# A two-layer hybrid decoder trunk in float32 on one core: the elementwise work leaves GpSimd, norm sums and gate results are placed between weight splits, and two raw weight buffers are added

## The chip, the core and the metric

The kernel runs on one core of a Trainium2 chip. A core has a matrix engine (TensorE, PE; its weight loads are listed apart as PEld), a vector engine (VectorE, DVE), an engine for activations, casts and copies (ScalarE, ACT) and a general engine (GpSimd, POOL). SyncE (SP) here only issues DMA transfers. Each engine works through its own list of instructions in a fixed order and waits, by semaphores, for results of others. The metric is device time in microseconds for one launch.

## The reference

The input is `x` of 256 positions by 2048 channels, float32. Two layers follow one another; layer 0 mixes tokens with a state-space scan (SSD), layer 1 with forgetting attention (FoX). In both, the rest is the same:

```python
h = h + rmsnorm(mix, norm_mix_post[i])
ff = swiglu(rmsnorm(h, norm_ffn_pre[i]), ffn_w_gate[i], ffn_w_up[i], ffn_w_down[i])
h = h + rmsnorm(ff, norm_ffn_post[i])
pe = rmsnorm(p[i] @ ple_w_proj[i], ple_norm[i])
h = h + jax.nn.sigmoid(h @ ple_w_gate[i]) * pe
```

`swiglu` is `(silu(h @ w_gate) * (h @ w_up)) @ w_down` with 5632 hidden channels; `rmsnorm` divides by the root of the mean square over the channels and multiplies by a gain. The per-layer embedding (PLE) has 256 channels. Every weight is read once.

## The kernel before

**Layout.** Channels lie on the 128 partitions, positions along the free axis: `h` is 16 tiles (chunks) of 128 x 256. A float32 product is made of three passes. A weight `raw` is split into a high part `wh` (a cast on ACT, L174) and a low part `wl = raw - wh` (DVE, L176); an activation `x` likewise into two halves that lie beside each other (`split`: the high half on ACT, L261 or L264, the low half on DVE, L262 or L265). For each weight tile PE then does one pass of `wh` over both halves (512 columns, L233) and one of `wl` over the high half (256 columns, L235). `gather` (L256 on ACT, L257 on DVE) adds the two halves of an accumulator.

**Stages and units.** All weights are cut, ahead of time, into a list of stages of 128 x 640 to 128 x 1024. `emit_stage` makes a stage's DMA, cast and low part. `wh` and `wl` have four buffers each (`WB`), so stage i+4 can be cast only when PE has left stage i; `raw` has four (`RAWB`). `unit` runs one group of output tiles over all chunks of the contraction, looks `LOOK` = 2 stages ahead, and after each stage takes one entry (`pops`) from the queue `bg` of deferred work. At a unit's end it calls `evac` for each accumulator. The scheduler then fixes the order on each engine; `issue_after` pins an instruction behind another on that order. An accumulator has one of six buffers, so a unit of six tiles takes all of them.

**FFN.** `tail` runs per layer. Behind the mixer, `post_norm` makes the norm's scale. The first gate unit (stages 242 to 257 in layer 0, six tiles, 768 wide, one chunk a stage) is run while `mk_update` makes its inputs: per chunk c a scaled product `sg` or `pn` (L414), `h[c] += ` that (L422 on DVE, L424 on POOL for even c from 4), the split into `x` (L264, L265), and the square of `h` (ACT, L273) added to `ssb` on POOL (L274). At its end `mk_r` makes the norm scale of `ssb`: a matmul with ones (L280), `pow` on POOL (L287), a diagonal (`dg`, L293), a matmul (L296) that spreads it to `rwide` and `rwide2`. Each gate tile is then gathered into `sg`, multiplied by `rwide2` (L487), passed through tanh (L489), multiplied (L490) and scaled by `rwide` (L491). The up unit follows (stages 258 to 273), whose tiles are gathered into `g`, multiplied by `sg` (L506) and split into `a`, the input of the down product. Sums `ssp` of the squares of `pp`, the embedding's projection, run between stages by `bg`.

**PLE.** After the down products a second update without gain makes the gate product's input in its first unit. The four units have 6, 4, 4 and 2 tiles (`OUT0`). `e3` closes a tile as soon as its unit ends: gather, tanh (L553), `pp` times `rpe` on POOL (L537), `(1+th)*pp` (L555), residual into `h` (L556); then in layer 0 the split `xb` for the next layer and the square's sum on POOL, in layer 1 the output's DMA on SP.

**After layer 0** come five units for the values of FoX with tokens on the output partitions (`tok`); the first ends with `mk_r` on `ssb`.

Of the kernel before, what the change touches and what calls it, by code (L numbers as in the profile page):

```python
# [56 lines left out]
def tile_trunk(ctx, tc, a, out):  # L57
# [99 lines left out]
    def emit_stage(a_ins=None, v_ins=None):  # L157
# [15 lines left out]
        with after(a_ins):  # L173
            A.copy(out=wh[:, :kc * n], in_=raw[:, :kc * n])  # L174
        with after(v_ins):
            V.tensor_tensor(out=wl[:, :kc * n], in0=raw[:, :kc * n],  # L176
                            in1=wh.bitcast(F32)[:, :kc * n], op=sub)
# [90 lines left out]
    def sumsq(acc, src, first, eng=None):  # L268
        if first:
            return A.activation(acc, src, AF.Square)  # L270
        else:
# [1 line left out]
            mark[0] = r = A.activation(sq, src, AF.Square)  # L273
            (eng or V).tensor_tensor(out=acc, in0=acc, in1=sq, op=add)  # L274
            return r

# [124 lines left out]
    def mk_update(new, m, wpost, wpre, xs):
# [15 lines left out]
        def up(c):  # L417
            if c == 0:
                chain(lambda: scaled(0))
            e = G if H_POOL_EVERY and c >= 3 and c % H_POOL_EVERY == 0 else V  # L420
            if e is V:
                chain(lambda: V.tensor_tensor(out=h[c], in0=h[c], in1=ts[c], op=add))  # L422
            else:
                G.tensor_tensor(out=h[c], in0=h[c], in1=ts[c], op=add)  # L424
# [42 lines left out]
    def tail(i, mpx, m, pp, mk_next):  # L467
# [3 lines left out]
        with ExitStack() as st:  # L471
# [7 lines left out]
            def ev_g(t, acc):  # L479
                if first[0]:  # L480
                    bg.append(noop)
                    for c in range(8):
                        bg.append(lambda c=c: late_ssp(pp, c))
                    first[0] = False
                sg = new_sg()
                gather(acc, sg)
# [44 lines left out]
        def mkpe():  # L531
            rs = rstd_small(ssp, D)
            rstd_wide(rs, rpe)
            V.tensor_scalar(out=rpe, in0=rpe, scalar1=0.5, scalar2=None, op0=mult)

        def mkpp(c):
            G.tensor_tensor(out=pp[c], in0=pp[c], in1=rpe, op=mult)  # L537

        def ssq2():
            for c in range(8, NCH):  # L540
                late_ssp(pp, c, G)

        c_sep = NCH - OUT0[-1]

        def e3(t, acc, c0):
            c = c0 + t
# [9 lines left out]
            V.scalar_tensor_tensor(out=h[c], in0=pe, scalar=col(f"ple{i}", c), in1=h[c], op0=mult,  # L556
                                   op1=add)
# [538 lines left out]
```

## Time and profile before

| | us |
|---|---|
| median of 3 runs | 2797.61 (2797.36 to 2799.33) |
| profiled execution | 2800.33 |
| its span | 2798.5 |
| PE busy | 2768.2 (99%) |
| DVE busy | 1926.0 (69%) |
| ACT busy | 1484.8 (53%) |
| POOL busy | 183.5 (7%), 236 instructions |

A profile is of one execution; its span begins at the first instruction on the core, its time is that of the whole launch. In a group's row stand line, engine, operation, output and inputs, shape and count, then busy time, mean of one in ns, and the idle time just ahead with what ended it. In a timeline's row stand start, duration and instruction, with the idle time ahead in brackets and its releaser where there was one. A window's row gives busy time (and the number of instructions) of PE, PEld, DVE, ACT and POOL, the share of full clock that PE was granted, the DMA engines' share and GB/s. Ends of matmuls are modelled, so times of PE are best read from start to start.

### The profile page before, as it was taken

How to read it: one execution, taken by the hardware profiler on the slowest of the kernel's cores; microseconds unless marked ns; L12 is line 12 of the kernel's file. 1: busy time of each engine (PE TensorE's matmuls, PEld its weight loads, DVE VectorE, ACT ScalarE, POOL GpSimd, SP SyncE). 2: the span in 40 equal slices, each digit the busy share in tenths (PEclk: the TensorE clock that was granted, in tenths of full speed). 3: DMA queues.
4: the chain of work that ended last, by engine and by line, in shares of the span. 5: the costliest groups of instructions: out<-in, count | busy, mean ns of one | idle time of the engine just before them, and what ended most of it. 6: DMA issues, size and time to landing. Idle time of an engine off the chain costs nothing.

```text
span 2798.5 us, 43191 instructions
## 1 busy us (share of the span) xinstructions
PE 2768.2 (99%) x16306; PEld 2447.5 (87%) x16306; DVE 1926.0 (69%) x3033; ACT 1484.8 (53%) x2455; POOL 183.5 (7%) x236
## 2 busy tenths in 40 slices
PE   9999999999999999999999999999999999999999
PEld 8888888889788888888897998888888888888888
DVE  8888888855966645666669656766866545666577
ACT  6587676644654444444446544555654444445454
POOL 2000000000300000000005000000200000000022
PEclk9999999999999999999999999999999999999999
DMA  7666665565566656666555676655666556656545
GB/s 235 189 197 183 194 191 177 158 202 180 161 201 189 192 191 188 188 180 194 194 168 167 189 207 191 178 161 166 181 189 192 192 190 187 195 172 204 192 153 176
DMA packets 262512, 520.09 MB, mean 186 GB/s; under 512 B 17392, under 2 KB 42128, under 8 KB 262304
## 3 DMA queue, kind: packets, MB, share of 16 engines
q1 hardware_dynamic: 258640, 504.96, 58.8%
q0 software_dynamic: 3520, 12.15, 1.5%
q8 instruction: 127, 2.08, 0.3%
q14 instruction: 81, 0.66, 0.1%
q10 hardware_dynamic: 144, 0.24, 0.0%
HBM read 515.10 MB, written 2.18 MB: 185 GB/s over the span
## 4 chain that ended last, share of the span: by engine, by line
PE 91%; DVE 4%; issue 4%; ACT 1%; POOL 0%; DMA 0%; DVEq 0%; ACTq 0%; POOLq 0%
PE acc L233 53%; PE acc L235 28%; PE acc L230 1%; PE acc L229 1%; PE acc L228 1%; PE acc L223 1%; PE acc L222 1%; PE acc L224 1%; PE mi L751 1%; DVE x L265 1%; DVE wl L176 1%; DVE sg L414 1%; DVE x L262 0%; DVE h L422 0%; PE mi L753 0%
## 5 line engine op out<-in xcount | busy, mean ns | idle before, releaser
L233 PE MATMUL acc<-x,wh 128*128 128x512 f32 x5008 | 1718.9, 394 | 13.7 <-DVE x L265 6.6
L176 DVE TENSOR_TENSOR wl<-raw,wh 128x1024 fp32r<-128x1024 f32 (+4 forms) x1020 | 1183.2, 1166 | 782.4 <-ACT wh L174 778.8
L174 ACT CAST wh<-raw 128x1024 fp32r<-128x1024 f32 (+4 forms) x1020 | 1006.6, 993 | 989.0 <-PE acc L233 809.9
L235 PE MATMUL acc<-x,wl 128*128 128x256 f32 x5008 | 1340.0, 283 | 7.5 <-DVE wl L176 7.5
L233 PEld LDWEIGHTS acc<-x,wh 128*128 128x128 f32 x5008 | 928.2, 188 | 209.5 <-DVE x L265 14.7
L235 PEld LDWEIGHTS acc<-x,wl 128*128 128x128 f32 x5008 | 932.5, 189 | 33.1 <-DVE wl L176 10.9
L233 PE MATMUL acc<-a,wh 128*128 128x512 f32 x1232 | 425.5, 391 | 0.0
L235 PE MATMUL acc<-a,wl 128*128 128x256 f32 x1232 | 341.9, 282 | 0.0
L233 PEld LDWEIGHTS acc<-a,wh 128*128 128x128 f32 x1232 | 229.9, 188 | 47.1
L235 PEld LDWEIGHTS acc<-a,wl 128*128 128x128 f32 x1232 | 232.6, 189 | 2.2
L233 PE MATMUL acc<-xb,wh 128*128 128x512 f32 x512 | 181.9, 396 | 0.0
L256 ACT COPY tb<-acc 128x256 f32<-128x256 f32 (+1 forms) x401 | 139.6, 369 | 38.6 <-PE acc L235 19.0
L235 PE MATMUL acc<-xb,wl 128*128 128x256 f32 x512 | 145.8, 285 | 0.0
L287 POOL TENSOR_TENSOR rs<-ms,mhalf 128x2 f32<-128x2 f32 x18 | 21.2, 1177 | 1752.8 <-DVE ms L284 1752.8
L233 PEld LDWEIGHTS acc<-xb,wh 128*128 128x128 f32 x512 | 95.9, 188 | 19.3
L235 PEld LDWEIGHTS acc<-xb,wl 128*128 128x128 f32 x512 | 96.7, 189 | 0.7 <-issue 0.2
L257 DVE TENSOR_TENSOR g<-acc,tb 128x256 f32<-128x256 f32 x204 | 78.7, 415 | 2.1 <-ACT tb L256 1.6
L233 PE MATMUL acc<-xq,wh 128*128 128x512 f32 x224 | 77.6, 390 | 0.0
L733 ACT ACTIVATE E<-ab,bias 128x128 f32<-128x128 f32 x192 | 59.8, 390 | 15.3 <-PE mi L753 14.7
L661 DVE SCALAR_TENSOR_TENSOR g<-xr,vec,g 128x256 f32<-128x256 f32 x144 | 62.4, 476 | 4.0 <-ACT g L658 3.5
L235 PE MATMUL acc<-xq,wl 128*128 128x256 f32 x224 | 62.8, 282 | 0.0
L274 POOL TENSOR_TENSOR ssb<-ssb,sqp 128x256 f32<-128x256 f32 x60 | 55.5, 925 | 61.2 <-ACT sqp L273 56.7
...
## 6 DMA issues: line engine op xcount, KB each, us to landing
raw<-down SPq DMA_DIRECT2D x176, 512.0 KB, 4.1
...
raw<-gate SPq DMA_DIRECT2D x128, 512.0 KB, 3.9
raw<-up SPq DMA_DIRECT2D x128, 512.0 KB, 4.5
...
```

The lines of the kernel that those rows point to most:

```text
L174: A.copy(out=wh[:, :kc * n], in_=raw[:, :kc * n])
L176: V.tensor_tensor(out=wl[:, :kc * n], in0=raw[:, :kc * n], in1=wh.bitcast(F32)[:, :kc * n], op=sub)
L222: PE.matmul(o, lhsT=xh, rhs=wh[:, c, :], start=st, stop=False)
L223: PE.matmul(o, lhsT=xh, rhs=wl[:, c, :], start=False, stop=False)
L224: PE.matmul(o, lhsT=x[:, 1, t * P:(t + 1) * P], rhs=wh[:, c, :], start=False, stop=sp)
L233: PE.matmul(accs[t], lhsT=wh[:, c, t * P:(t + 1) * P], rhs=x.rearrange("p a n -> p (a n)"), start=st, stop=False)
L235: PE.matmul(accs[t][:, :T], lhsT=wl[:, c, t * P:(t + 1) * P], rhs=x[:, 0, :], start=False, stop=sp)
L256: A.copy(out=tb[:np_], in_=acc[:np_, T:2 * T])
L257: V.tensor_tensor(out=o, in0=acc[:np_, :T], in1=tb[:np_], op=add)
L274: (eng or V).tensor_tensor(out=acc, in0=acc, in1=sq, op=add)
L661: V.scalar_tensor_tensor(out=c, in0=xr[:, k:k + T], scalar=col(f"conv_w{k}", cc), in1=c, op0=mult, op1=add)
L733: A.activation(E[:, i, b * P:(b + 1) * P], ab[:, i, lo:lo + P], AF.Relu, scale=-1.0, bias=bias3[:, b, h0 + i:h0 + i + 1])
```

## The change

POOL keeps `pow`, memsets and DMA issues. Its sums (`ssb`, `ssp`), its adds to `h` and its products `pp * rpe` go to DVE. The sums of the first FFN norm no longer run with the update: `late_norm` puts them in `bg` in groups of 3, 3, 3, 4 and 3, then the two steps of the scale, then the gate's tanh and products in three pairs, all into the up unit that follows the first gate unit. `paced` pins such a group behind the latest `wl`, and `turn` pins the next `wl` behind the group. The `ssp` sums of the first eight tiles move behind that unit. In PLE, `e3` only gathers into `gz` (ten buffers), and `close` is taken from `bg` in later units, one per `wl`; the last unit closes its tiles at once. The `ssb` sums for FoX run within its first value unit, two per stage. `RAWB` goes from 4 to 6; a smaller scratch for descriptors makes room.

```diff
-RAWB = 4
+RAWB = 6
+SCRATCH = 8192
...
-H_POOL_EVERY = 2
...
+    low, turn = [None], [None]
...
+        if v_ins is None:
+            v_ins, turn[0] = turn[0], None
         with after(v_ins):
-            V.tensor_tensor(out=wl[:, :kc * n], in0=raw[:, :kc * n],
-                            in1=wh.bitcast(F32)[:, :kc * n], op=sub)
+            low[0] = V.tensor_tensor(out=wl[:, :kc * n], in0=raw[:, :kc * n],
+                                     in1=wh.bitcast(F32)[:, :kc * n], op=sub)
...
-    def sumsq(acc, src, first, eng=None):
+    def sumsq(acc, src, first):
...
+            sq = tmp("sq", bufs=4)
             mark[0] = r = A.activation(sq, src, AF.Square)
-            (eng or V).tensor_tensor(out=acc, in0=acc, in1=sq, op=add)
+            last_v[0] = V.tensor_tensor(out=acc, in0=acc, in1=sq, op=add)
...
+    def sums_of(acc, src, cs, by=(2,) * 8):
+        cs = list(cs)
+        return [lambda cc=[cs.pop(0) for _ in range(n)]: [paced(sumsq, acc, src[i], i == 0)
+                                                          for i in cc] for n in by]
+
+    def paced(f, *args):
+        with tc.issue_after(low[0].ins):
+            f(*args)
+        turn[0] = last_v[0]
...
-            e = G if H_POOL_EVERY and c >= 3 and c % H_POOL_EVERY == 0 else V
-            if e is V:
-                chain(lambda: V.tensor_tensor(out=h[c], in0=h[c], in1=ts[c], op=add))
-            else:
-                G.tensor_tensor(out=h[c], in0=h[c], in1=ts[c], op=add)
+            chain(lambda: V.tensor_tensor(out=h[c], in0=h[c], in1=ts[c], op=add))
...
-            am = mark[0]
-            if wpre is not None:
-                sumsq(ssb, h[c], c == 0, G)
...
+            def late_norm():
+                f1, f2 = mk_r()
+                bg.extend(sums_of(ssb, h, range(NCH), (3, 3, 3, 4, 3)))
+                bg.extend((noop, f1, noop, noop, f2, noop))
+                for j in range(0, len(sgs), 2):
+                    bg.append(lambda ss=sgs[j:j + 2]: paced(lambda: [silu(x) for x in ss]))
...
-        def mkpp(c):
-            G.tensor_tensor(out=pp[c], in0=pp[c], in1=rpe, op=mult)
...
+        def close(c, src):
             th = tmp("th")
-            if c >= c_sep:
-                A.activation(th, acc[:, :T], AF.Tanh, scale=0.5)
-            else:
-                g0 = tmp("g0")
-                gather(acc, g0)
-                A.activation(th, g0, AF.Tanh, scale=0.5)
+            A.activation(th, src, AF.Tanh, scale=0.5)
             pe = pp[c]
+            V.tensor_tensor(out=pe, in0=pe, in1=rpe, op=mult)
             V.scalar_tensor_tensor(out=pe, in0=th, scalar=1.0, in1=pe, op0=add, op1=mult)
...
+        def e3(t, acc, c0):
+            c = c0 + t
+            gz[c] = pn.tile([P, T], F32, tag="gz", name=nm("gz"), bufs=10)
+            gather(acc, gz[c])
...
+            if u == 0:
+                bg.extend(sums_of(ssp, pp, range(8, NCH), (1, 1, 2, 1, 2, 1)))
+                bg.extend((noop, pe_small, noop, noop, pe_wide))
+            if not last:
+                for c in range(c0, c0 + n):
+                    bg.append(lambda c=c: paced(close, c, gz[c]))
+                    if c < 2:
+                        bg.append(noop)
...
+    v1, v2 = mk_r(False, rsm)
+    bg.extend(sums_of(ssb, h, range(NCH)))
     for u in range(5):
-        unit(lambda k: nxt[k], ev_v(u), tok=True, late=mk_r(False, rsm) if u == 0 else ())
+        unit(lambda k: nxt[k], ev_v(u), tok=True, pops=2 if u == 0 else 1,
+             late=(lambda: (drain(), v1()), v2) if u == 0 else ())
```

Three places show how instructions stand. The rows give line, operation, output and inputs, and shape; a number behind `wl`, `wh` and `raw` is the stage. Lines of the changed kernel differ a little: L178 is `wl`, L267 the low half of `x`, L432 the add to `h`, L426 the scaled product.

First, DVE in the FFN update of layer 0. Before (`x_715` belongs to chunk 6, `x_717` to chunk 8, whose stages are 248 and 250):

```order
L176 TENSOR_TENSOR wl249_7954<-raw249_7951,wh249_7953 128x768
L265 SCALAR_TENSOR_TENSOR x_715_7674<-h6_89,vec_79,x_715_7674 128x256
L422 TENSOR_TENSOR h7_90<-h7_90,sg_778_7932 128x256
L414 SCALAR_TENSOR_TENSOR sg_780_7958<-m0_8_6591,vec_79,rwide_138 128x256
L176 TENSOR_TENSOR wl250_7980<-raw250_7977,wh250_7979 128x768
L265 SCALAR_TENSOR_TENSOR x_716_7675<-h7_90,vec_79,x_716_7675 128x256
L414 SCALAR_TENSOR_TENSOR sg_782_7984<-m0_9_6592,vec_79,rwide_138 128x256
L265 SCALAR_TENSOR_TENSOR x_717_7676<-h8_91,vec_79,x_717_7676 128x256
```

and in the changed kernel:

```order
L178 TENSOR_TENSOR wl249_7935<-raw249_7932,wh249_7934 128x768
L267 SCALAR_TENSOR_TENSOR x_714_7673<-h5_88,vec_79,x_714_7673 128x256
L432 TENSOR_TENSOR h6_89<-h6_89,sg_772_7893 128x256
L426 SCALAR_TENSOR_TENSOR sg_773_7916<-m0_7_6590,vec_79,rwide_138 128x256
L178 TENSOR_TENSOR wl250_7958<-raw250_7955,wh250_7957 128x768
L267 SCALAR_TENSOR_TENSOR x_715_7674<-h6_89,vec_79,x_715_7674 128x256
L432 TENSOR_TENSOR h7_90<-h7_90,sg_773_7916 128x256
L426 SCALAR_TENSOR_TENSOR sg_774_7939<-m0_8_6591,vec_79,rwide_138 128x256
```

The add to `h` stands in every chunk, and the `wl` ahead of a chunk's `x` is that of two stages later (250 ahead of `x_715`, stage 248), where it was one later.

Second, the end of the first up unit of layer 0, whose last stage is 273; stage 274 is the next gate unit's first. DVE before:

```order
L176 TENSOR_TENSOR wl271_8517<-raw271_8514,wh271_8516 128x768
L176 TENSOR_TENSOR wl272_8535<-raw272_8532,wh272_8534 128x768
L176 TENSOR_TENSOR wl273_8553<-raw273_8550,wh273_8552 128x768
L176 TENSOR_TENSOR wl274_8571<-raw274_8568,wh274_8570 128x1024
L176 TENSOR_TENSOR wl275_8577<-raw275_8574,wh275_8576 128x1024
L257 TENSOR_TENSOR g0_833_8604<-acc_820_8288,tb_834_8605 128x256
L257 TENSOR_TENSOR g0_835_8611<-acc_821_8289,tb_836_8612 128x256
L506 TENSOR_TENSOR g0_833_8604<-g0_833_8604,sg_802_8234 128x256
```

DVE in the changed kernel (`sg_790` and `sg_792` are the last two of the six gate tiles, `acc_794` and `acc_795` the first two of the up unit):

```order
L178 TENSOR_TENSOR wl273_8521<-raw273_8518,wh273_8520 128x768
L485 TENSOR_TENSOR sg_790_8189<-sg_790_8189,rwide2_139 128x256
L485 TENSOR_TENSOR sg_792_8193<-sg_792_8193,rwide2_139 128x256
L488 SCALAR_TENSOR_TENSOR sg_790_8189<-th_824_8537,sg_790_8189 128x256
L259 TENSOR_TENSOR g0_826_8582<-acc_794_8197,tb_827_8583 128x256
L489 TENSOR_TENSOR sg_790_8189<-sg_790_8189,rwide_138 128x256
L259 TENSOR_TENSOR g0_828_8589<-acc_795_8198,tb_829_8590 128x256
L525 TENSOR_TENSOR g0_826_8582<-g0_826_8582,sg_782_8173 128x256
L488 SCALAR_TENSOR_TENSOR sg_792_8193<-th_825_8542,sg_792_8193 128x256
L525 TENSOR_TENSOR g0_828_8589<-g0_828_8589,sg_784_8177 128x256
L489 TENSOR_TENSOR sg_792_8193<-sg_792_8193,rwide_138 128x256
L178 TENSOR_TENSOR wl274_8549<-raw274_8546,wh274_8548 128x1024
```

and ACT in the changed kernel:

```order
L174 CAST wh276_8630<-raw276_8628 128x1024
L174 CAST wh277_8652<-raw277_8650 128x1024
L487 ACTIVATE th_824_8537<-sg_790_8189 128x256
L258 COPY tb_827_8583<-acc_794_8197 128x256
L258 COPY tb_829_8590<-acc_795_8198 128x256
L487 ACTIVATE th_825_8542<-sg_792_8193 128x256
```

The gate products of the last pair and two gathers stand ahead of `wl274`, and the tanh of that pair stands on ACT behind the casts of stages 276 and 277.

Third, DVE in layer 0's third PLE unit, in the changed kernel (before, the closes of a unit's tiles stood together at its end, with two or three of their instructions between two `wl`):

```order
L259 TENSOR_TENSOR gz_1323_15733<-acc_1301_15487,tb_1324_15734 128x256
L259 TENSOR_TENSOR gz_1325_15737<-acc_1302_15488,tb_1326_15738 128x256
L267 SCALAR_TENSOR_TENSOR xb_1236_14978<-h0_83,vec_79,xb_1236_14978 128x256
L178 TENSOR_TENSOR wl548_15670<-raw548_15667,wh548_15669 128x1024
L564 TENSOR_TENSOR pp0_1_6600<-pp0_1_6600,rpe_142 128x256
L565 SCALAR_TENSOR_TENSOR pp0_1_6600<-th_1317_15689,pp0_1_6600 128x256
L566 SCALAR_TENSOR_TENSOR h1_84<-pp0_1_6600,vec_79,h1_84 128x256
L267 SCALAR_TENSOR_TENSOR xb_1237_14979<-h1_84,vec_79,xb_1237_14979 128x256
L178 TENSOR_TENSOR wl549_15699<-raw549_15696,wh549_15698 128x1024
```

A whole close, with the split `xb` for the next layer, stands between two `wl`, and the last gathers of the unit before stand ahead of `wl548`.

More of the change, by code (lines that the diff above doesn't have):

```diff
@@ L244, in unit @@
             evac(t, accs[t])
-    mark, dmark = [None], [None]
+    mark, dmark, last_v = [None], [None], [None]
     def tmp(tag, shape=(P, T), dt=F32, bufs=2):
@@ L477, in tail, with silu @@
             first = [True]
[L479 to L486, printed above, removed]
+            def silu(sg):
                 V.tensor_tensor(out=sg, in0=sg, in1=rwide2, op=mult)
@@ L490, in ev_g @@
                 V.scalar_tensor_tensor(out=sg, in0=th, scalar=1.0, in1=sg, op0=add, op1=mult)
-                V.tensor_tensor(out=sg, in0=sg, in1=rwide, op=mult)
+                last_v[0] = V.tensor_tensor(out=sg, in0=sg, in1=rwide, op=mult)
+            def ev_g(t, acc):
+                sg = new_sg()
+                gather(acc, sg)
                 sgs.append(sg)
+                if not first[0]:
+                    silu(sg)
+            def late_norm():
[4 more added lines that the diff above has]
+                    bg.append(lambda ss=sgs[j:j + 2]: paced(lambda: [silu(x) for x in ss]))
             for half in range(2):
@@ L499, in tail, with ev_u @@
                     up = mk_update(new_sg, m, f"mix_post{i}", f"ffn_pre{i}", xs) if first[0] else None
-                    unit(lambda k: xs[k], ev_g, pre=up, late=mk_r() if first[0] else (),
-                         look=0 if first[0] else LOOK)
-                    def ev_u(t, acc, c0=c0, acts=acts):
+                    unit(lambda k: xs[k], ev_g, pre=up, look=0 if first[0] else LOOK)
+                    begun = first[0]
+                    first[0] = False
+                    if begun:
+                        late_norm()
+                    def ev_u(t, acc, c0=c0, acts=acts, begun=begun):
+                        if begun and t == 0:
+                            drain()
+                            bg.append(noop)
+                            for c in range(8):
+                                bg.append(lambda c=c: late_ssp(pp, c))
                         up = tmp("g0")
@@ L529, in tail, with pe_small, pe_wide @@
         post_norm(filler(pp, (2, 3)))
[L531 to L533 removed]
+        def pe_small():
+            r_pe.append(rstd_small(ssp, D))
+        def pe_wide():
+            rstd_wide(r_pe[0], rpe)
             V.tensor_scalar(out=rpe, in0=rpe, scalar1=0.5, scalar2=None, op0=mult)
[L536 to L553 removed]
+        r_pe = []
+        gz = {}
+        def close(c, src):
+            th = tmp("th")
+            A.activation(th, src, AF.Tanh, scale=0.5)
             pe = pp[c]
+            V.tensor_tensor(out=pe, in0=pe, in1=rpe, op=mult)
             V.scalar_tensor_tensor(out=pe, in0=th, scalar=1.0, in1=pe, op0=add, op1=mult)
[L556 to L557 removed]
+            last_v[0] = V.scalar_tensor_tensor(
+                out=h[c], in0=pe, scalar=col(f"ple{i}", c), in1=h[c], op0=mult, op1=add)
             if next_xs is None:
@@ L560, in e3, with e3_last @@
             else:
-                split(h[c], next_xs[c], col("mix_pre1", c))
-                sumsq(ssb, h[c], c == 0, G)
+                last_v[0] = split(h[c], next_xs[c], col("mix_pre1", c))
+        def e3(t, acc, c0):
+            c = c0 + t
+            gz[c] = pn.tile([P, T], F32, tag="gz", name=nm("gz"), bufs=10)
+            gather(acc, gz[c])
+        def e3_last(t, acc, c0):
+            close(c0 + t, acc[:, :T])
         c0 = 0
@@ L589, in prep0 @@
         split(h[c], xs0[c], col("mix_pre0", c))
-        sumsq(ssb, h[c], c == 0, G)
+        sumsq(ssb, h[c], c == 0)
     with ExitStack() as ys:
```

27 lines of the change are left out of this document (12 added, 15 removed).

## The prediction

> **What bounds the kernel now.** I read the page's busy shares first, then the waits of PE by releaser, then the windows around the places with waits.
>
> ```profile
> PE 2768.2 (99%) x16306; PEld 2447.5 (87%) x16306; DVE 1926.0 (69%) x3033; ACT 1484.8 (53%) x2455; POOL 183.5 (7%) x236
> PE acc L235 <- DVE wl L176: 7.5, 7, 1.8
> PE acc L233 <- DVE x L265: 6.6, 11, 1.5
> PE acc L233 <- DVE x L262: 3.7, 8, 0.8
> PE mi L296 <- DVE dg L293: 3.4, 4, 0.9
> ```
>
> PE is the bound: 2768.2 of 2798.5 us. The rows of waits (total us, times, longest) say that whatever PE waits for comes from DVE: low halves `wl` of the weights, and split activations `x`. These three rows hold 17.8 us; the `dg` chain is not touched. More than that can hardly be won, plus pipeline refill and clock.
>
> ```profile
> 0.00:35.00 35.00, 31.24 (x159) 26.53 (x160) 26.93 (x37) 24.97 (x52) 14.82 (x23) 0.95 0.81 259
> 701.00:746.00 45.00, 40.63 (x226) 33.28 (x225) 43.01 (x66) 28.11 (x58) 22.18 (x23) 1.00 0.54 142
> 1459.00:1482.00 23.00, 20.98 (x115) 17.34 (x114) 22.81 (x34) 13.31 (x27) 14.77 (x13) 1.00 0.49 142
> 1521.50:1525.00 3.50, 3.50 (x14) 2.98 (x13) 3.50 (x7) 3.00 (x8) 3.31 (x2) 0.51 0.58 189
> 1944.00:1991.00 47.00, 42.65 (x239) 35.06 (x238) 44.86 (x71) 30.10 (x63) 22.69 (x23) 1.00 0.54 147
> 2755.00:2762.00 7.00, 5.59 (x31) 4.43 (x29) 7.00 (x7) 2.74 (x4) 5.76 (x6) 1.00 0.48 150
> ```
>
> The columns after the width are busy PE, PEld, DVE, ACT, POOL, then clock share. In the two FFN updates (701 and 1944) DVE is busy 43.01 of 45 us and 44.86 of 47, with POOL at work beside it. In those stretches DVE is the bound, not PE.
>
> ```profile
> L274 POOL TENSOR_TENSOR ssb<-ssb,sqp 128x256 f32<-128x256 f32 x60 | 55.5, 925 | 61.2 <-ACT sqp L273 56.7
> L537 POOL TENSOR_TENSOR pp<-pp,rpe 128x256 f32<-128x256 f32 x32 | 31.6, 1025 | 12.4 <-DVE rpe L534 12.4
> L424 POOL TENSOR_TENSOR h<-h,pn 128x256 f32<-128x256 f32 x12 | 17.8, 1485 | 33.0 <-ACT x L261 22.0 <-DVE pn L414 11.0
> L424 POOL TENSOR_TENSOR h<-h,sg 128x256 f32<-128x256 f32 x12 | 16.6, 1387 | 18.7 <-DVE sg L414 18.7
> L274 POOL TENSOR_TENSOR ssp<-ssp,sqp 128x256 f32<-128x256 f32 x16 | 15.3, 959 | 2.5 <-ACT sqp L273 1.7
> 711.30 0.94 DVE L265 SCALAR_TENSOR_TENSOR x<-h,vec,x 128x256 fp32r<-128x256 f32 x1
> 712.17 0.41 DVE L422 TENSOR_TENSOR h<-h,sg 128x256 f32<-128x256 f32 x1
> 712.50 0.47 DVE L414 SCALAR_TENSOR_TENSOR sg<-m,vec,rwide 128x256 f32<-128x256 f32 x1
> 712.90 0.95 DVE L176 TENSOR_TENSOR wl<-raw,wh 128x768 fp32r<-128x768 f32 x1
> 713.77 0.96 DVE L265 SCALAR_TENSOR_TENSOR x<-h,vec,x 128x256 fp32r<-128x256 f32 x1
> ```
>
> **The work that comes to DVE.** The five POOL groups are 132 instructions. A 256-wide add takes DVE 0.41 alone (712.17), so 132 x 0.41 = 54 us of new DVE work in 2798. In exchange, instructions that overlap POOL shrink: a scaled op is 0.94 at 711.30 and 0.47 at 712.50. The five rows add to 136.8 us; if DVE runs at half speed beside all of it, it gets back 68 us, if beside two thirds, 46. The totals about cancel, so it is the place that decides. Start to start, the clean rows give 0.33 for an add, 0.40 for a scaled op, 0.87 for a 768-wide `wl`.
>
> **FFN update, both layers (gain).**
>
> ```profile
> 712.30 0.50 PE L233 MATMUL acc<-x,wh 128*128 128x512 f32 x1 [1.54 <-DVE x L265]
> 721.71 0.50 PE L233 MATMUL acc<-x,wh 128*128 128x512 f32 x1 [0.33 <-DVE x L265]
> 741.46 0.50 PE L233 MATMUL acc<-x,wh 128*128 128x512 f32 x1 [0.34 <-DVE x L265]
> 770.66 0.39 PE L233 MATMUL acc<-x,wh 128*128 128x512 f32 x1
> 772.74 0.39 PE L233 MATMUL acc<-x,wh 128*128 128x512 f32 x1
> 715.20 0.82 ACT L174 CAST wh<-raw 128x768 fp32r<-128x768 f32 x1
> 713.06 1.39 POOL L424 TENSOR_TENSOR h<-h,sg 128x256 f32<-128x256 f32 x1 [1.09 <-DVE sg L414]
> ```
>
> An undisturbed stage of six tiles is 772.74 - 770.66 = 2.08, or 0.347 a tile. From 712.30 to 741.46 lie 12 stages: 29.16 against 25.0, so 4.2 lost; with the first stall of 1.54, its refill, and the start, about 6.3 a layer. Every second `h` is on POOL at 1.39 where DVE takes 0.41, and the `x` of that chunk comes later by as much. Now a chunk costs DVE `sg` 0.40 + `h` 0.33 + `wl` 0.87 + `x` 0.40 = 2.0, just under 2.08. But the order puts `wl` of chunk c+2 ahead of `x` of chunk c, and its `wh` needs the slot of stage c-2. From the end of that stage: cast 0.82 (715.20), `wl` 0.87, `x` 0.47, hand-overs 0.14, so 2.3. Two stages then take 2.08 + 2.3, 2.2 each: 0.11 lost a chunk, 1.5 over 13; of the first stall about 1.1 stays, 1.54 less what one contended `x` (0.94 for 0.47) gives back. Gain 6.3 - 2.6 = 3.7 a layer, **-7.4** (bounds 0, if the loop holds, to -12.6). The norm matmul that sat behind POOL's last sum frees 0.7 a layer, **-1.4** (bounds 0 and -1.4); three sums before each `wl` (3 x 0.41 + 0.87 = 2.10 against 2.08, plus waits for squares) cost 0.5, **+1.0** (bounds 0 and +3).
>
> **End of the first up unit (loss).** The gate results are now pairs between `wl` 271 to 274.
>
> ```profile
> 774.21 1.05 ACT L174 CAST wh<-raw 128x1024 fp32r<-128x1024 f32 x1 [1.25 <-PE acc L233]
> 776.28 1.05 ACT L174 CAST wh<-raw 128x1024 fp32r<-128x1024 f32 x1 [1.03 <-PE acc L233]
> 777.92 0.65 ACT L256 COPY tb<-acc 128x256 f32<-128x256 f32 x2 [0.58 <-PE acc L235]
> 775.28 1.22 DVE L176 TENSOR_TENSOR wl<-raw,wh 128x1024 fp32r<-128x1024 f32 x1 [1.33 <-ACT wh L174]
> 778.51 0.75 DVE L257 TENSOR_TENSOR g<-acc,tb 128x256 f32<-128x256 f32 x2
> L489 ACT ACTIVATE th<-sg 128x256 f32<-128x256 f32 x88 | 32.8, 420 | 41.3 <-DVE sg L487 38.8 <-DVE sg L490 2.5
> ```
>
> The casts wait for PE to leave a slot (releaser PE). In the old order nothing but its cast and earlier `wl` stood ahead of `wl` 274. In the new one the last pair's first tanh stands behind the casts `wh` 276 and 277 on ACT, and `wh` 277 needs the slot that stage 273 reads. Counted from PE's last read of `wh` 273: cast 1.05 and tanh 0.42 end at about 1.5; two copies `tb` (0.65 the pair) then the second tanh at 2.35. On DVE eight instructions stand from the first of these products to `wl` 274 (two `(1+th)*sg`, two gathers, two times `rwide`, two times the up result), 0.35 apart: 1.5 + 2.8 = 4.3, and `wl` 274, 1.22, ends at 5.5. PE has six `wl` passes of stage 273 left after that read (0.7, a third of a stage) and two `wh` 274 passes (0.46) before it needs `wl` 274, part of them waiting for a gather: it resumes 5.5 - 1.16 = 4.3 late, in two pieces of about 1.7 and 2.2. I take 4.4 with a small delay of `wl` 273: **+8.8** in two layers (bounds 0, if PE is that far behind anyway, and +12).
>
> **PLE updates (gain).** Window 1459 shows 2.02 idle of 23. In the FFN update 6.3 lost stand against 4.37 - 0.86 = 3.5 idle (window 701, less the `dg` wait), 1.8 times as much, so 3.6 here. The same loop without POOL, as above, leaves about half: **-3.6** in two layers (bounds 0 and -6.8).
>
> **PLE closes.** Tanh, product, residual and, in layer 0, the split for the next layer now come one per `wl` of a later unit.
>
> ```profile
> 1517.31 0.39 PE L235 MATMUL acc<-x,wl 128*128 128x256 f32 x1 [1.75 <-DVE wl L176]
> 1520.98 0.39 PE L235 MATMUL acc<-x,wl 128*128 128x256 f32 x1 [1.78 <-DVE wl L176]
> 1519.72 1.21 DVE L176 TENSOR_TENSOR wl<-raw,wh 128x1024 fp32r<-128x1024 f32 x1
> L264 ACT ACTIVATE xb<-h,vec 128x256 fp32r<-128x256 f32 x16 | 8.0, 505 | 11.2 <-DVE h L556 11.0
> ```
>
> Before, layer 0 loses 1.75 + 1.78 + refill, and half of the 3.5 us at clock 0.51: 5.6. After, the chain between two `wl`, each waiting for the one ahead with 0.04 of hand-over, is product 0.45, `(1+th)*pp` 0.45, `h` 0.51, ACT `xb` 0.55, DVE `xb` 0.40, `wl` 1.14 (1.21 less overlap): 3.5, against a stage of eight tile passes x 0.347 = 2.78. Seven stages lose 0.72 each, 5.0. Ahead of them `wl` 548 waits for gathers whose copy stands behind `wh` 551, a cast that needs stage 547's slot: 1.05 + 0.37 + 0.42 + 0.40 + 1.22 = 3.46 after that stage against 0.92 of cover, 2.5; after them 2.5 more until the lead is back. Together 10: **+4.4** (bounds -5.6 and +8). Layer 1 has no split: 0.45 + 0.45 + 0.40 + 1.14 = 2.44 fits in 2.78, so of the 1.4 idle in window 2755 and its refills **-1.0** goes (bounds +2 and -2). Its output transfers keep their place and number on SP, at nothing; the last ones still follow the last `h`. The token-major unit after layer 0 gets 16 sums and the last splits: 8 stages with little idle today, **+0.5** (bounds 0 and +3).
>
> **Start.**
>
> ```profile
> 22.72 1.13 PE L235 MATMUL acc<-x,wl 128*128 128x256 f32 x5 [1.76 <-DVE wl L176]
> ```
>
> This stall and the lowered clock behind it (0.95 over 35 us is 1.75) come from a DVE that shares its time with POOL. Six raw buffers let two more weight loads stand ahead; SP issues them two loads of `x` earlier, so each of those tiles comes later by one transfer, while DVE is still chunks behind. Later on the casts wait for PE's slots (774.21, 776.28), not for `raw`, so there they are worth nothing. DVE then needs `wl` 0.75 + `x` 0.40 + sum 0.41, 1.6 a chunk: **-3.0** (bounds 0 and -4).
>
> **Clock.** After idles of 1.76 (22.72) and of 1.75 and 1.78 (1517, 1521) the share halves for some 3.5 us, 1.7 lost; after 1.54 (712.30) it does not. The two new boundary stalls are of the first kind, so **+3.4** (bounds 0 and +5.1, with layer 0's closes). The Trainium skill, "TensorE: Matmul & The Clock Gate", Part 1, lets the clock fall only after an idle window of about 3.4 us; by it these broken stalls would cost no clock and the sum would be 3.4 lower. The trace has it fall after shorter ones, so the trace decides.
>
> **Sum.** -7.4 - 1.4 + 1.0 + 8.8 - 3.6 + 4.4 - 1.0 + 0.5 - 3.0 + 3.4 = +1.7. The profiled run took 2800.33 (span 2798.5 and 1.8 around it), so 2802.0 there; it is 2.7 above the median of 2797.61, from which I forecast 2799.3, called **2799**.
>
> **Rivals.** (1) The deferred groups are hidden: DVE, idle 31%, has run far enough ahead, and neither boundary nor closes lose more than now. For it: `wl` at 775.28 ends at 776.5, while its stage starts one stage after 776.28, at 778.4. Against: that lead is lost once a tanh stands behind a slot-bound cast. Boundary, clock and the +4.4 fall away: 1.7 - 8.8 - 3.4 - 4.4 = -14.9, **2783**. (2) Slower: the update loop doesn't shorten. `x` stays behind a `wl` that waits for PE's own lateness; if the period stays above 2.5 us a chunk, as in 29.16/12 = 2.43 now, the 7.4 and 3.6 are lost: 1.7 + 11.0 = +12.7, **2810**. For it: DVE's 2.0 leaves 0.08 of room. Against: half of today's `x` are slow only beside POOL. (3) The change doesn't do what it says: the pins move nothing that binds, the stalls only change their releaser, **2798**.
>
> **Chances.** Forecast 0.43, own range 2791 to 2805; rival 1 0.30, rival 2 0.17, rival 3 0.10. About 0.2% (5.6 us) is what a measurement here can tell from no change. Faster by more: 0.30 + 0.04 of the forecast + 0.03 = 0.37; within: 0.33 + 0.04 = 0.37; slower: 0.17 + 0.06 + 0.03 = 0.26. The range, 2782 to 2810, ends within rival 1 and at the middle of rival 2, and leaves out about half of each.
>
> **What would show it.** Right: in the updates no `x` wait over 0.3 but the first; a wait for `wl` of about 2 us and one for the gather at the end of each first up unit, with the clock at 0.5 behind; stages of about 3.5 us in layer 0's third PLE unit; the `wl` wait near 20 us gone. Wrong: PE idle near 0 at these boundaries (rival 1), or `x` waits of 0.3 in every other chunk (rival 2).

## The result and the profile after

The changed kernel takes 2818.11 us (median of 4 runs, 2817.89 to 2818.49) against 2797.76 for the one before: a ratio of 1.0072, 95% interval 1.0054 to 1.0089. It is 20 us slower, where 2799 was forecast and the range ended at 2810.

The page's busy shares of the changed kernel:

```profile
PE 2778.6 (99%) x16306; PEld 2450.3 (87%) x16306; DVE 1917.2 (68%) x3165; ACT 1485.1 (53%) x2455; POOL 48.8 (2%) x104
```

POOL's 132 instructions moved and DVE's busy time did not rise: 1926.0 before, 1917.2 now. In total the move cost nothing, as forecast. What PE waits for (total us, times, longest):

```profile
PE acc L237 <- DVE wl L178: 8.9, 11, 2.4
PE acc L235 <- DVE x L267: 3.6, 13, 1.0
...
PE acc L225 <- DVE wl L178: 3.1, 5, 1.2
PE acc L235 <- DVE g L259: 2.9, 4, 1.3
PE acc L235 <- DVE gz L259: 1.8, 2, 0.9
PE acc L235 <- DVE x L264: 1.8, 4, 0.6
```

The waits for `x` are halved (10.3 us before, 5.4 now), and waits for `wl` and for gathers have come in their place: 13.6 for `wl` with the 1.6 of one at L232, 4.7 for gathers.

**Where the time went.** Both kernels run the same matmuls of the units in the same sequence. So the start of the n-th one in one trace, less that in the other, says how much has been lost up to there, lost clock included. The table gives the change of that difference over each stretch, against the profiled execution of the kernel before. Columns: the changed kernel, then runs told of below (pairs three stages earlier; pairs unpinned; split free; both of these; no pins; pins in PLE only).

| us against before | changed | earlier | pairs | split | both | none | PLE only |
|---|---|---|---|---|---|---|---|
| start, to the first FFN | -3.1 | -2.9 | -4.8 | -3.0 | -4.9 | -4.4 | -2.9 |
| first gate units, two layers | -6.3 | -6.2 | -6.3 | -6.2 | -6.2 | -4.9 | -4.9 |
| first up units | +2.5 | +4.6 | +2.6 | +2.5 | +2.6 | +0.9 | +0.9 |
| their ends | +13.9 | +12.7 | +2.6 | +14.0 | +2.6 | +0.1 | +0.1 |
| first PLE unit, layer 0 | +0.1 | +0.1 | +0.1 | +0.1 | +0.1 | +6.6 | +0.1 |
| other PLE units, layer 0 | +5.6 | +5.6 | +5.6 | -2.2 | -2.2 | -5.5 | +0.8 |
| first value unit | +4.4 | +4.4 | +4.4 | +2.4 | +2.4 | 0.0 | 0.0 |
| PLE, layer 1 | 0.0 | 0.0 | 0.0 | 0.0 | 0.0 | +3.5 | 0.0 |
| all, to the last matmul | +17.2 | +18.2 | +4.4 | +7.7 | -5.4 | -3.6 | -6.0 |
| median of the runs | 2818.1 | 2818.1 | 2805.1 | 2806.5 | 2795.4 | 2796.0 | 2793.0 |

The sums contain 0.1 to 0.2 from between the stretches. The row of the ends begins some four stages before the unit's end and reaches into the next gate unit; the row of layer 1's PLE holds its update and its closes. The row of the start is not one to compare runs by: in the first 600 us the engines run the same instructions in the same order in the changed kernel and in the runs of columns 2 to 5 and 7, and their starts lie between -2.9 and -4.9. Three stretches make the loss: the ends of the first up units, the PLE units behind the update in layer 0, and the value unit behind them.

**End of the first up unit**, changed kernel, timeline of PE, DVE and ACT (start, us, instruction, idle ahead and releaser):

```profile
775.16 0.97 PE L237 MATMUL acc<-x,wl 128*128 128x256 f32 x6 [0.23 <-DVE wl L178]
777.40 0.50 PE L235 MATMUL acc<-x,wh 128*128 128x512 f32 x1 [1.27 <-DVE g L259]
778.06 0.80 PE L235 MATMUL acc<-x,wh 128*128 128x512 f32 x1 [0.17 <-DVE g L259]
780.54 0.58 PE L237 MATMUL acc<-x,wl 128*128 128x256 f32 x1 [1.68 <-DVE wl L178]
...
776.58 0.42 DVE L488 SCALAR_TENSOR_TENSOR sg<-th,sg 128x256 f32<-128x256 f32 x1 [0.80 <-ACT th L487]
779.26 2.35 DVE L178 TENSOR_TENSOR wl<-raw,wh 128x1024 fp32r<-128x1024 f32 x2
...
775.18 1.05 ACT L174 CAST wh<-raw 128x1024 fp32r<-128x1024 f32 x1 [1.16 <-PE acc L235]
776.14 0.41 ACT L487 ACTIVATE th<-sg 128x256 f32<-128x256 f32 x1
```

The cast at 775.18 is `wh` 277 and waits for PE; the tanh comes behind it at 776.14, DVE waits 0.80 for the tanh, eight instructions follow, and `wl` 274 starts at 779.26, 4.1 after the cast (forecast 4.3). PE loses 4.5 by its start times. In this stall the clock falls, as the windows show (busy PE, PEld, DVE, ACT, POOL, clock share, DMA share, GB/s):

```profile
770.00:780.50 10.50, 7.19 (x35) 5.22 (x33) 8.26 (x20) 6.67 (x14) 0.00 (x0) 0.88 0.35 101
780.50:784.00 3.50, 3.46 (x11) 2.98 (x12) 3.50 (x4) 0.00 (x0) 0.00 (x0) 0.50 0.61 171
1521.50:1525.00 3.50, 3.49 (x13) 3.16 (x14) 2.85 (x6) 1.51 (x4) 0.00 (x0) 0.57 0.43 150
```

**PLE closes, layer 0**, same kernel, timeline:

```profile
1521.51 0.39 PE L237 MATMUL acc<-x,wl 128*128 128x256 f32 x1 [2.43 <-DVE wl L178]
1549.86 0.38 PE L232 MATMUL acc<-x,wl 128*128 128x256 f32 x1 [1.59 <-DVE wl L178]
...
1520.24 1.22 DVE L178 TENSOR_TENSOR wl<-raw,wh 128x1024 fp32r<-128x1024 f32 x1
1521.38 0.42 DVE L564 TENSOR_TENSOR pp<-pp,rpe 128x256 f32<-128x256 f32 x1
...
1523.35 0.49 DVE L267 SCALAR_TENSOR_TENSOR xb<-h,vec,xb 128x256 fp32r<-128x256 f32 x1 [0.58 <-ACT xb L266]
1523.75 1.22 DVE L178 TENSOR_TENSOR wl<-raw,wh 128x1024 fp32r<-128x1024 f32 x1
```

From `wl` to `wl` it is 3.51 (forecast 3.5), of which 0.58 is DVE idle for ACT's half of `xb`. The first stall is 2.43; another of 1.59 comes in the last PLE unit (L232), where two gathers stand in the chain as well.

**The value unit**, same kernel, timeline:

```profile
1570.77 1.01 DVE L178 TENSOR_TENSOR wl<-raw,wh 128x824 fp32r<-128x824 f32 x1
1571.69 2.01 DVE L276 TENSOR_TENSOR ssb<-ssb,sq 128x256 f32<-128x256 f32 x4
1573.62 1.01 DVE L178 TENSOR_TENSOR wl<-raw,wh 128x824 fp32r<-128x824 f32 x1
```

Four sums, each waiting for the one before, take 2.01 and stand between two `wl`, which are 2.85 apart. (There are four and not two to a stage: an entry of the queue holds two sums, and this unit takes two entries a stage.) In the same unit of the kernel before, where DVE has little else to do, the timeline of DVE shows the `wl` 2.24 apart:

```profile
1566.57 1.02 DVE L176 TENSOR_TENSOR wl<-raw,wh 128x824 fp32r<-128x824 f32 x1 [1.18 <-ACT wh L174]
1568.81 1.02 DVE L176 TENSOR_TENSOR wl<-raw,wh 128x824 fp32r<-128x824 f32 x1 [1.22 <-ACT wh L174]
```

So a stage with four sums is 0.6 longer on DVE than the stage of the unit.

**The updates**, same kernel, timeline:

```profile
712.79 0.50 PE L235 MATMUL acc<-x,wh 128*128 128x512 f32 x1 [0.16 <-DVE x L267]
717.39 0.50 PE L235 MATMUL acc<-x,wh 128*128 128x512 f32 x1 [0.16 <-DVE x L267]
1489.38 0.50 PE L235 MATMUL acc<-x,wh 128*128 128x512 f32 x1 [0.59 <-DVE x L264]
1494.72 0.50 PE L235 MATMUL acc<-x,wh 128*128 128x512 f32 x1 [0.92 <-DVE gz L259]
...
1492.77 1.23 DVE L178 TENSOR_TENSOR wl<-raw,wh 128x1024 fp32r<-128x1024 f32 x1 [1.38 <-ACT wh L174]
1493.91 0.42 DVE L276 TENSOR_TENSOR ssp<-ssp,sq 128x256 f32<-128x256 f32 x1
1494.25 0.75 DVE L259 TENSOR_TENSOR gz<-acc,tb 128x256 f32<-128x256 f32 x2
```

In the FFN update two stages take 4.60 where 4.17 is undisturbed. In PLE the next unit's first matmul waits for the gather `gz`, ahead of which a `wl` and a pinned sum stand on DVE.

### The profile page after: what moved, and what is told of

It reads as the page before. It is cut to its first block, busy times and chain, and to the rows that moved or that the text cites. A ratio compares the mean times of both kernels' runs of the same rounds, so it can differ in the third digit from the quotient of the medians.

```text
span 2816.1 us, 43112 instructions
## 1 busy us (share of the span) xinstructions
PE 2778.6 (99%) x16306; PEld 2450.3 (87%) x16306; DVE 1917.2 (68%) x3165; ACT 1485.1 (53%) x2455; POOL 48.8 (2%) x104
## 3 DMA queue, kind: packets, MB, share of 16 engines
q8 instruction: 127, 2.08, 0.3%
## 4 chain that ended last, share of the span: by engine, by line
PE 95%; DVE 3%; issue 1%; ACT 1%; DMA 0%; POOL 0%; DVEq 0%; SPq 0%; ACTq 0%; POOLq 0%
PE acc L235 55%; PE acc L237 29%; PE acc L232 1%; PE acc L230 1%; PE acc L231 1%; DVE wl L178 1%; PE acc L224 1%; PE acc L225 1%; PE acc L226 1%; PE mi L773 1%; PE mi L775 0%; ACT wh L174 0%; PE mi L308 0%; PE mi L292 0%; PE mi L740 0%
## 5 line engine op out<-in xcount | busy, mean ns | idle before, releaser
L178 DVE TENSOR_TENSOR wl<-raw,wh 128x1024 fp32r<-128x1024 f32 (+4 forms) x1020 | 1171.2, 1154 | 781.5 <-ACT wh L174 780.0
L755 ACT ACTIVATE E<-ab,bias 128x128 f32<-128x128 f32 x192 | 59.7, 390 | 17.2 <-PE mi L775 16.1
L259 DVE TENSOR_TENSOR g<-acc,tb 128x256 f32<-128x256 f32 x176 | 67.3, 416 | 0.3
L225 PE MATMUL acc<-wl,xb 128*128 128x412 f32 (+1 forms) x160 | 56.6, 353 | 3.1 <-DVE wl L178 3.1
L276 DVE TENSOR_TENSOR ssb<-ssb,sq 128x256 f32<-128x256 f32 x120 | 50.5, 421 | 12.6 <-ACT sq L275 8.6
```

Source lines behind the costliest of these rows:

```text
L178: low[0] = V.tensor_tensor(out=wl[:, :kc * n], in0=raw[:, :kc * n], in1=wh.bitcast(F32)[:, :kc * n], op=sub)
L225: PE.matmul(o, lhsT=xh, rhs=wl[:, c, :], start=False, stop=False)
L259: V.tensor_tensor(out=o, in0=acc[:np_, :T], in1=tb[:np_], op=add)
L276: last_v[0] = V.tensor_tensor(out=acc, in0=acc, in1=sq, op=add)
L755: A.activation(E[:, i, b * P:(b + 1) * P], ab[:, i, lo:lo + P], AF.Relu, scale=-1.0, bias=bias3[:, b, h0 + i:h0 + i + 1])
```

## The experiments

The theory that these set out from is the forecast's own: a `wl` that stands behind a result of ACT, itself queued behind a cast that waits for PE, stalls PE. The rival is that DVE now has too much to do in those stretches, in whatever order.

**Gate results three stages earlier.**

```diff
-                bg.extend(sums_of(ssb, h, range(NCH), (3, 3, 3, 4, 3)))
-                bg.extend((noop, f1, noop, noop, f2, noop))
+                bg.extend(sums_of(ssb, h, range(NCH), (4, 4, 4, 4)))
+                bg.extend((f1, noop, f2, noop))
```

> Norm sums of the first FFN norm in groups of 4, 4, 4, 4 and fewer empty slots, so that the three pairs of gate products stand three stages earlier (ahead of wl 269, 270 and 271 instead of 272, 273 and 274); the work is the same. Theory (the last pair's tanh stands on ACT behind casts that wait for PE to leave the last stage of the unit, and wl 274 stands behind that pair): the 6.6 us at the end of each first up unit (4.5 of stall and the clock behind it) go, 13 us in all, and the time falls from 2818 to about 2805. Rival 1 (the pairs cost DVE time wherever they stand: three chains of 2.9 us against stages of 2.09, 2.4 a layer): the stall moves three stages forward and shrinks to 2.4, about 2810. Rival 2 (the stall is that of the gathers and of six accumulators in use, not of the tanh): no change, 2818.

Measured: 2818.09, no change. What the end of the unit gave back was lost in the paired stages ahead of it. Timeline of DVE and PE in this run:

```profile
766.53 0.95 DVE L178 TENSOR_TENSOR wl<-raw,wh 128x768 fp32r<-128x768 f32 x1
768.83 0.76 DVE L488 SCALAR_TENSOR_TENSOR sg<-th,sg 128x256 f32<-128x256 f32 x2 [0.68 <-ACT th L487]
770.18 0.95 DVE L178 TENSOR_TENSOR wl<-raw,wh 128x768 fp32r<-128x768 f32 x1
772.61 0.76 DVE L488 SCALAR_TENSOR_TENSOR sg<-th,sg 128x256 f32<-128x256 f32 x2 [0.81 <-ACT th L487]
773.96 0.95 DVE L178 TENSOR_TENSOR wl<-raw,wh 128x768 fp32r<-128x768 f32 x1
...
767.54 0.98 PE L237 MATMUL acc<-x,wl 128*128 128x256 f32 x6 [0.79 <-DVE wl L178]
771.19 0.97 PE L237 MATMUL acc<-x,wl 128*128 128x256 f32 x6 [1.27 <-DVE wl L178]
782.16 0.50 PE L235 MATMUL acc<-x,wh 128*128 128x512 f32 x1 [2.03 <-DVE g L259]
```

The three `wl` are 3.65 and 3.78 apart, against stages of 2.08. By start times the three paired stages of layer 0 lose 4.3 (0.4 in the changed kernel) and the end of the unit, to the first stage of the next, 2.3 (6.4 there). The number is the one of rival 2, its reason only in part. PE waits for `wl` in each paired stage, and DVE itself waits for the tanh; but the 2.03 that are left at the end are a wait for a gather, which DVE reaches only behind seven `wl` in a row. The pin closes a loop, `wl` to PE to slot to cast to tanh to product to the next `wl`, in both places tried. As written, the theory's remedy was wrong.

**Gate results unpinned.**

```diff
-                    bg.append(lambda ss=sgs[j:j + 2]: paced(lambda: [silu(x) for x in ss]))
+                    bg.append(lambda ss=sgs[j:j + 2]: [silu(x) for x in ss])
```

> The three pairs of gate results stay in their slots of the first up unit, but nothing is pinned: neither the pair behind a wl nor the next wl behind the pair. Theory, as mended after the run with earlier pairs (the pin closes a loop: a wl waits for the pair ahead of it, the pair for a tanh behind a cast, the cast for PE to leave a slot, PE for an earlier wl, so that every paired stage takes 3.7 us in place of 2.08 wherever the pairs stand): the stall at the end of the first up unit falls from 4.5 to under 1.5 and the clock stays up, 11 to 13 less in two layers, 2805 to 2807. Rival (tanh and products are too much for DVE and ACT in that stretch in any order): 4 or less is won, 2814 or more.

Measured: 2805.13, ratio 1.0023 (1.0014 to 1.0033), 13 less than the changed kernel with the same work. The ends of the up units cost 2.6 in place of 13.9. Timeline of this run:

```profile
774.50 0.50 PE L235 MATMUL acc<-x,wh 128*128 128x512 f32 x1 [0.60 <-DVE g L259]
...
769.07 1.22 DVE L178 TENSOR_TENSOR wl<-raw,wh 128x1024 fp32r<-128x1024 f32 x1
```

`wl` 274 is made at 769.07, over five us ahead of its use at 774.5. The rival falls for this stretch.

**Gate results one by one, in two steps, pins kept** (with the split free).

```diff
-                bg.extend((noop, f1, noop, noop, f2, noop))
...
+                bg.extend((f1, noop, f2))
...
+                def step(j):
+                    if j:
+                        silu_b(sgs[j - 1])
+                    if j < n:
+                        silu_a(sgs[j])
+                for j in range(n + 1):
+                    bg.append(lambda j=j: paced(step, j))
```

`silu_a` is the first product and the tanh, `silu_b` the two products behind it. The two steps of the norm scale lose three of their four empty slots, so the first tile comes sooner behind the scale.

> Pins kept, but the gate results one tile per slot and in two steps: product and tanh in one slot, the two products behind the tanh in the next, so that no wl is pinned behind a tanh of its own slot; the split xb free as well. Theory (a wl may stand behind DVE work but not behind a result that ACT makes after a cast): as with the pairs unpinned, 2793 to 2797. Rival (any pin there costs a stage): 2800 to 2806.

Measured: 2798.80, ratio 1.0001 (0.9991 to 1.0010), between the two expectations. Up units and their ends cost 8.6 in the two layers, against 5.2 with the pairs unpinned. Neither DVE nor a `wl` waits for a tanh here any more. The one wait for `wl` that is left in this stretch of layer 0 (0.90, at 765.96) has another cause: the first product is pinned, and DVE stands 4.56 idle ahead of it for ACT's copy of the norm scale. At the end of the unit PE waits 1.17 for a gather (0.60 with the pairs unpinned). What the pins and what the fewer empty slots cost was not tried apart.

**Split of the PLE closes not pinned.**

```diff
-                last_v[0] = split(h[c], next_xs[c], col("mix_pre1", c))
+                split(h[c], next_xs[c], col("mix_pre1", c))
```

> In the PLE closes of layer 0 the split xb for the next layer is no longer what the next wl is pinned behind; the wl is pinned behind the residual into h alone, and the split falls where there is room. The work is the same. Theory (the chain product, (1+th)*pp, h, ACT xb, DVE xb, wl takes 3.5 us between two wl where a stage is 2.78): without ACT's copy and the wait for it 2.6 to 2.7 are left, the seven stages lose nothing and the first stall of 2.4 goes with the gathers that stood ahead of wl 548; 6 to 8 less, 2810 to 2812. Rival (DVE has too much work there in any order, and what is not lost in PLE is lost in the value unit): at most 2 less, 2816 to 2818.

Measured: 2806.51, ratio 1.0028 (1.0017 to 1.0039), 11.6 less. Timeline of DVE:

```profile
1521.86 1.22 DVE L178 TENSOR_TENSOR wl<-raw,wh 128x1024 fp32r<-128x1024 f32 x1
1523.00 0.42 DVE L564 TENSOR_TENSOR pp<-pp,rpe 128x256 f32<-128x256 f32 x1
1523.33 0.48 DVE L267 SCALAR_TENSOR_TENSOR xb<-h,vec,xb 128x256 fp32r<-128x256 f32 x1
1523.73 0.42 DVE L565 SCALAR_TENSOR_TENSOR pp<-th,pp 128x256 f32<-128x256 f32 x1
...
1524.59 1.22 DVE L178 TENSOR_TENSOR wl<-raw,wh 128x1024 fp32r<-128x1024 f32 x1
```

The same five instructions now fit in 2.73, since the split of one tile falls into the next tile's chain and ACT has had its time. The gain is 7.8 in PLE and 2.0 in the value unit, which no longer inherits late closes; the second part was not expected.

**Sums of the value unit back on POOL.** Each sum stands on POOL behind the split of its tile.

> Only the 16 sums of squares for the FoX norm go back to POOL, each right behind the split of its tile, out of the first value unit. Theory (in that unit DVE has two sums, the last splits and a wl per stage, more than a stage of 2.24 us, and this costs the 4.3 us that the changed kernel loses there): the unit gives back about 4, the closes lose 0 to 2 to POOL beside them, 2814 to 2816. Rival (the loss is the backlog of the closes, not the sums): the loss stays, 2818 to 2820.

Measured: 2823.25, slower by 5. Timeline of this run, DVE and POOL:

```profile
1538.40 1.22 DVE L178 TENSOR_TENSOR wl<-raw,wh 128x1024 fp32r<-128x1024 f32 x1
1539.54 0.96 DVE L566 TENSOR_TENSOR pp<-pp,rpe 128x256 f32<-128x256 f32 x1
1542.46 1.22 DVE L178 TENSOR_TENSOR wl<-raw,wh 128x1024 fp32r<-128x1024 f32 x1
...
1538.42 1.80 POOL L276 TENSOR_TENSOR ssb<-ssb,sq 128x256 f32<-128x256 f32 x1 [2.26 <-ACT sq L275]
```

One POOL sum makes one product 0.96 where it is 0.42, and the chain 4.06 where it is 3.51: the PLE units lose 9.5 in place of 5.6, and their backlog the value unit 7.5, most of it in one wait of 4.05 for a `wl` that stands behind the late closes, with the clock at half behind it. So this run could not part sums from backlog; the run with the split free and the run without pins do.

**Both edits: pairs unpinned, split free.**

> The two edits together: pairs not pinned, and the split xb of the PLE closes not what the next wl is pinned behind. Theory (both losses are made by pins, in different stretches): the gains add, 11.6 and 11 to 13, 2793 to 2796, 2 to 5 faster than the kernel before. Rival (the stalls share a cause or one hides the other): 2800 or more.

Measured: 2795.39, ratio 0.9988 (0.9978 to 0.9997). The gains add (13.0 + 11.6 = 24.6 expected, 22.7 measured), and the time is 0.1% below the kernel before. That is no proof that the work is better placed on DVE: the kernel before with six raw buffers (below) stands at 0.9991, which the intervals do not tell from this.

**No pins at all.** In `paced` only the call `f(*args)` is left.

> Every group of deferred work keeps its slot, but none is pinned: sums, gate results and closes fall where the scheduler sets them. Theory (the pins, not the move of the work to DVE, make the loss): FFN boundaries and the value unit give back 13 and 4, the closes, now bunched ahead of a few wl, lose about what they lost before; 2796 to 2801. Rival (DVE is overloaded by the work that came from POOL, pinned or not): 2810 or more.

Measured: 2796.02, ratio 0.9989 (0.9979 to 0.9998). Every slot is as in the changed kernel and the 22 us are gone. The value unit costs nothing, so its 4.4 were the pins: 2.0 of late closes (split free) and 2.4 of the sums' own. But the first PLE units lose 6.6 and 5.7. The waits of PE and the timeline of DVE:

```profile
PE acc L235 <- DVE x L264: 11.2, 6, 4.0
```

```profile
1465.22 4.44 DVE L562 TENSOR_TENSOR pp<-pp,rpe 128x256 f32<-128x256 f32 x13
```

Without pins thirteen products slip, in one block of 4.44, ahead of a `wl` of the update. There a pin earns its place, as the next run bears out.

**Pins in PLE only** (sums of `pp` and closes, split free; nothing pinned in the FFN and the value unit).

> Pins are kept only where the unpinned run lost: for the sums of pp and for the closes in PLE (with the split xb free). FFN norm sums, gate results and the sums in the first value unit keep their slots but are not pinned. The work is the same as in the changed kernel. Theory (the pins lose in the FFN and the value unit and win in PLE, each by its own stretch): the start and the FFN as in the run without pins, PLE as with both edits, the value unit flat; 2786 to 2790, 0.3% or more under the kernel before. Rival (what a stretch loses or wins hangs on the neighbours, so the best parts don't add): 2793 or more.

Measured: 2793.04, ratio 0.9979 (0.9970 to 0.9988): the fastest by its median, 25 us under the changed kernel and 0.2% under the one before. (With equal numbers of raw buffers it is 3.7 under the kernel before with six, and 2.5 with four; see below.) But it is short of the expected 2786 to 2790, and the rival's number is met. The best parts did not all add: the other PLE units show +0.8 where they had -2.2, and the waits name the place:

```profile
PE acc L232 <- DVE wl L178: 1.6, 1, 1.6
```

L232 is in the last PLE unit. The value unit's sums, unpinned, slip among the closes ahead of it: with one `ssb` sum between them the `wl` of the third PLE unit are 2.9 to 3.3 apart, where they are 2.73 in the run with both edits and a stage is 2.78. The start (-2.9 here, -4.4 in the run without pins) explains nothing, since it differs as much between runs with the same instructions there.

**Raw buffers**, in three kernels: the changed one with four, the last one with four, and the kernel before with six.

```diff
-RAWB = 6
+RAWB = 4
```

> Four raw buffers in place of six, all else as changed. Theory (the gain of 3 us in the first 35 us comes from POOL no longer slowing DVE): within 0.5 of 2818. Rival (it comes from the weights being loaded earlier): the gain goes, 2821, with the wait for wl near 20 us back.

> The kernel of the run with pins in PLE only, with four raw buffers in place of six. Theory (DVE and PE's slots set the pace, not the loads): within 1 us of that run. Rival (the two buffers carry gain wherever DVE and ACT run unevenly): 2 to 4 us slower than it.

> The kernel before, with six raw buffers and the smaller scratch as its only edit; POOL keeps its work. Theory (the 3 us gained in the first 35 us come from POOL leaving DVE alone): the wait for wl near 20 us stays, and the time is within 1 us of the kernel before. Rival (they come from the earlier loads): 2 to 4 us less.

Measured: 2820.04 (against 2818.11 with six; by the ratios to the kernel before, 1.0075 and 1.0072, only 0.8 apart), 2796.44 (against 2793.04, ratios 0.9991, 0.9982 to 1.0000, and 0.9979), 2796.75 (against 2798.95 with four, ratio 0.9991, 0.9982 to 0.9999). Each time six is the faster, by 1.9, 3.4 and 2.2; the first is not told apart from nothing, the others are at the edge of what the intervals tell. By the profiles the start is 2.5 to 3.5 earlier in all three, with POOL at work and six buffers as well as without it and with four, and the wait of 1.76 near 20 us is in none of them. So my cause for the start is not borne out: either edit goes with the gain. The profiled execution of the kernel before took 2800.33 where its runs have medians of 2797.8 to 2799.1, so part of its long start may be its own; that was not tried apart.

## Why the prediction was wrong

The stalls at the ends of the up units and in the PLE closes were those of the forecast; the sum came out wrong mainly through four terms (FFN updates, first up units, PLE updates, first value unit: 11.7 of the 15.5 below) and the base. By its terms, forecast and measured (table above):

- Ends of the first up units and clock, +12.2: 13.9. Right. The stall was 4.5 (forecast 4.4) and the clock fell; it cost about 2.5 each and not 1.7, since it stayed at half for 6.8 us at each, for part of which PE stood idle. (In layer 0 the shares of 0.88 and 0.50 above, and 0.90 in the 3.5 us behind them, add up to about that.)
- PLE closes of layer 0, +4.4: 5.6. Right in the mechanism, with 3.51 for the chain and 2.43 for the first stall. That the sum is near is in part luck: against 2.78 a stage, the seven stages behind the first lose 3.4 and not 5.0, and the first stage, where the clock falls too, loses 3.9 and not 2.5.
- FFN updates and norm matmul, -8.8: -6.3. The loop was right and its step mis-sized: 0.21 lost a chunk (4.60 against 4.17 for two), not 0.11. Of the 0.43 lost in two stages, 0.32 lie ahead of the matmul that waits, by its start (the row's idle of 0.16 goes by a modelled end), where the forecast had 0.22; 0.11 lie behind it (0.50 for 0.39), and this refill was left out of the term.
- First up units, +1.0: 2.5. What makes the difference stays open.
- PLE updates, -3.6 in two layers: +0.2, 0.1 in each. **This step failed.** The loop loses a little less than before, but the deferred sums and a `wl` stand ahead of the gathers at the unit's end, and the next unit waits 0.92 plus refill for a buffer; the last `x` waits 0.59. "About half" was taken over from the FFN without reading the order at the end of the unit.
- First value unit, +0.5: +4.4. **This step failed most.** "Little idle today" was read from the kernel before, and the same arithmetic that gave 3.5 for a close was not done for the four sums between `wl` (four take 2.01, and the `wl` are 2.85 apart against 2.24); nor was it asked where the late closes go, four of whose splits `xb` stand behind the unit's first `wl`. With nothing pinned there the unit loses 0.0.
- PLE closes of layer 1, -1.0: -0.1.
- Start, -3.0: -3.1 in the profile. As a term of the median it was probably counted twice: the sum was made from an execution that lay 2.7 above its median, and then these 2.7 were taken off again. That the 2.7 lie at the start is not shown.

The terms miss by 15.5 (1.7 against 17.2), the base by 2.7; the last 0.9 lies behind the last matmul and between one execution and the median. All errors but the start's have the same sign: gains were kept whole, and places where work comes to rest were called free. The rival on the slow side (update loop not shorter) is refuted, since the updates gained 6.3; the slow side came true through another mechanism that stood in the forecast with a price of 0.5. Rival 1 (the groups are hidden) is what the kernel does once those pins are gone, at 2795 to 2796, not 2783. Rival 3 (the pins move nothing) falls with the stalls above.

The clock: the Trainium skill, "TensorE: Matmul & The Clock Gate", Part 1, asks for an idle window of about 3.4 us. The forecast set the trace against it and was right here that shorter idles are enough: one of 2.43 was followed by a share of 0.57, and in the first stall the clock fell at 777.90, behind the wait of 1.27 and ahead of that of 1.68. But in the run with earlier pairs, waits of 0.79, 1.27 and 1.42 some 3.7 apart left it whole, and the same wait of 2.03 for a gather left it whole in layer 0 (ended at 782.16) and brought it down in layer 1 (ended at 2040.29):

```profile
782.00:785.50 3.50, 3.34 (x19) 2.97 (x20) 3.21 (x11) 2.40 (x8) 0.00 (x0) 1.00 0.99 373
2040.50:2044.00 3.50, 3.50 (x15) 2.98 (x15) 3.21 (x11) 2.50 (x8) 0.00 (x0) 0.65 1.01 382
```

So the length of an idle alone doesn't decide. By the traces' records of the granted clock, each fall ahead of the last matmul lasts 3.41 or 6.83 us, and within a trace the falls begin whole multiples of 3.413 us apart: at 777.90, 1522.00 and 2037.41 in the changed kernel (218 and 151 of them), at 1522.72 and 2041.55 in that run (152). So it seems to count where a stall lies against this grid; by what rule, these runs don't settle.

## What to carry to other kernels

An instruction that is pinned behind a group takes on everything that the group waits for; ask of each pin whether the group holds a result of another engine, and what that engine has queued ahead. A slot for deferred work and a pin are two things: the slots without pins did no harm at the boundaries and in the value unit, and pins paid only where independent work would have run ahead of a wait that counts. When work is deferred, cost the stretch where it lands with the same arithmetic as the one that it leaves.

## What had not been expected

The three pinned pairs cost about as much in either place tried, 16 to 17 us in two layers by the rows of the up units and their ends. A POOL add beside DVE did not slow all that DVE did: the `wl` at 1538.40 kept its 1.22 while the POOL sum begun 0.02 later took 1.80, and the next product took 0.96 where it is 0.42, as if the one that comes second waits. That fits the Trainium skill, "SBUF — State Buffer", section "Who interferes with whom": the pair of ports that DVE shares with GpSimd is held by one of them at a time. Sums that each need the one before took 0.50 apiece (2.01 for four), where independent adds start 0.33 apart.
